# One activation and one multiply per tile in the middle of a gated-SiLU kernel, and its last tile stored in two pieces

## Chip, cores, metric

The kernel runs on one core of one Trainium2 chip. The metric is the device time of one execution in microseconds (us). An execution of this kernel repeats within about 0.3%. Tiles, loads and stores are numbered from 0.

## The reference

```python
def reference(x):                       # x: 32 x 512 x 2048, float32
    x1, x2 = x[..., :1024], x[..., 1024:]
    return (x1 * (1 / (1 + np.exp(-x1)))) * x2     # silu(x1) * x2
```

134.2 MB are read and 67.1 MB are written. There is one activation and one multiply for each output element, and nothing is used twice.

## The kernel before

The 16,384 rows are cut into 16 tiles of 1,024 rows: 128 partitions, 8 rows each. A tile of the input is 8.4 MB, a tile of the output 4.2 MB. Both pools have two buffers. Loads are issued from the scalar engine's (ACT's) queue, stores from the sync engine's (SP's) queue. Both kinds share the same 16 DMA engines.

```python
    K = 8
    KC = 2
    ...
    in_pool = ctx.enter_context(tc.tile_pool(name="in_pool", bufs=2))
    out_pool = ctx.enter_context(tc.tile_pool(name="out_pool", bufs=2))
    ...
    load(0)
    load(1)
    for i in range(n_tiles):
        ...
        last = i == n_tiles - 1
        ot = out_pool.tile([P, K, half], dt, name="ot")
        for c in range(0, k, KC):
            ce = min(c + KC, k)
            nc.scalar.activation(
                out=ot[:, c:ce, :],
                in_=xt[:, c:ce, :half],
                func=mybir.ActivationFunctionType.Silu,
            )
            nc.vector.tensor_mul(
                out=ot[:, c:ce, :],
                in0=ot[:, c:ce, :],
                in1=xt[:, c:ce, half:],
            )
            if last:
                nc.sync.dma_start(out=ov[:, c:ce, :], in_=ot[:, c:ce, :])
        if not last:
            nc.sync.dma_start(out=ov, in_=ot[:, :k, :])
        if i + 2 < n_tiles:
            load(i + 2)
```

So each tile is computed in four chunks of 2 rows: while the vector engine (DVE) multiplies one chunk, ACT computes the next. The store of a tile and the load of the tile after next are issued when the last multiply of the tile is done. The last tile is stored chunk by chunk.

Of the kernel before, what the change touches and what calls it, by code (L numbers as in the profile page):

```python
# [1 line left out]

# [4 lines left out]


def issue_ahead_of_the_first_barrier(nc):




    head, body = nc.main_func.blocks[:2]
    load = next(ins for ins in body.instructions if type(ins).__name__ == "InstDMACopy")
    at = next(
        j for j, ins in enumerate(head.instructions)
        if ins.engine == load.engine and type(ins).__name__ == "InstDrain"
    )
    body.instructions = [ins for ins in body.instructions if ins.name != load.name]  # L20
    head.instructions = head.instructions[:at] + [load] + head.instructions[at:]


@with_exitstack
def kernel(
    ctx: ExitStack,
    tc: tile.TileContext,
    x: bass.AP,
    out: bass.AP,
):  # L30






    nc = tc.nc
    P = nc.NUM_PARTITIONS

    x_flat = x.flatten_outer_dims()  # L40
    out_flat = out.flatten_outer_dims()
    num_rows, in_cols = x_flat.shape
    half = in_cols // 2
    dt = x_flat.dtype

    K = 8
    KC = 2
    PLAN = [K] * (num_rows // (P * K))

    in_pool = ctx.enter_context(tc.tile_pool(name="in_pool", bufs=2))  # L50
    out_pool = ctx.enter_context(tc.tile_pool(name="out_pool", bufs=2))

    plan = []
    row = 0
    for k in PLAN:
        plan.append((row, k))
        row += P * k
    assert row == num_rows
    n_tiles = len(plan)

    def view(flat, i):
        row0, k = plan[i]
        return flat[row0:row0 + P * k].rearrange("(p k) d -> p k d", k=k)

    nc.at_finalize(issue_ahead_of_the_first_barrier)


    ctx.enter_context(tc.manual_schedule())

    loaded = {}  # L70

    def load(i):
        xt = in_pool.tile([P, K, in_cols], dt, name="xt")
        nc.scalar.dma_start(out=xt[:, :plan[i][1], :], in_=view(x_flat, i))
        loaded[i] = xt
# [4 lines that stand above are left out]
        k = plan[i][1]  # L80
        xt = loaded.pop(i)
        last = i == n_tiles - 1
        ov = view(out_flat, i)
        ot = out_pool.tile([P, K, half], dt, name="ot")
        for c in range(0, k, KC):
            ce = min(c + KC, k)
            nc.scalar.activation(  # L87
                out=ot[:, c:ce, :],
                in_=xt[:, c:ce, :half],
# [4 lines that stand above are left out]
                in0=ot[:, c:ce, :],  # L94
                in1=xt[:, c:ce, half:],
            )
            if last:
                nc.sync.dma_start(out=ov[:, c:ce, :], in_=ot[:, c:ce, :])
        if not last:
            nc.sync.dma_start(out=ov, in_=ot[:, :k, :])  # L100
        if i + 2 < n_tiles:
            load(i + 2)


# [1 line left out]
_INS = ['x']  # L106
_OUTS = [((32, 512, 1024), 'float32')]


# [23 lines left out]
```

## Time and profile before

| | before |
|---|---|
| time, median of the first 3 runs | 470.82 us (470.62 to 471.04) |
| span of the profiled execution | 468.9 us |
| DVE busy, ACT busy | 142.3 us, 118.2 us |
| moved by DMA | 201.3 MB, 429 GB/s over the whole span |

First the windows view of the kernel before. A row gives a stretch of time from the start of the span, its length, each engine's busy us and instructions, the clock, the share of the time in which the 16 DMA engines were busy, and GB/s.

```profile
core 0: us, DVE busy (x) ACT busy (x) POOL busy (x), PEclk, DMA share, GB/s
50.00:79.00 29.00, 8.90 (x5) 7.32 (x6) 0.00 (x0) 1.00 1.00 434
400.00:429.00 29.00, 9.00 (x5) 7.41 (x5) 0.00 (x0) 1.00 1.00 434
454.00:460.00 6.00, 6.00 (x4) 4.34 (x3) 0.00 (x0) 1.00 0.91 389
```

Read the last two columns first. In the middle of the kernel the DMA engines are busy the whole time, at 434 GB/s, while DVE works 9 and ACT 7 of each 29 us. One tile's load and store are 12.6 MB, and 12.6 MB at 434 GB/s are these 29.0 us. The third row is the tail, after the last load has landed. A packet seems to be counted whole in the window in which it starts, since short windows can show a share above 1; so a window of a few us is only good to about a tenth.

The groups of instructions of the kernel before (line, engine, operation, output from input, shapes, count, busy us, mean ns, idle time before them and what ended it):

```profile
L92 DVE TENSOR_TENSOR ot<-ot,xt 128x2048 f32<-128x2048 f32 x64 | 142.3, 2286 | 319.5 <-ACT ot L87 319.5
L87 ACT ACTIVATE ot<-xt 128x2048 f32<-128x2048 f32 x64 | 116.9, 1897 | 338.8 <-DMA xt<-in_x_dram 338.8
```

The DMA issues of the kernel before (output from input, queue, count, size of one, median us from issue to landing):

```profile
out_dram<-ot SPq DMA_DIRECT2D x15, 4096.0 KB, 39.8
...
xt<-in_x_dram ACTq DMA_DIRECT2D x16, 47.1
```

A load needs 47.1 us from issue to landing although only 29.0 us of transfer lie behind it. The other 18.1 us it waits in the queue behind the load before it. This is the slack of the loads.

From the page of the kernel before, the chain that ended last, by line:

```profile
DMA xt<-in_x_dram 80%; DVE ot L92 15%; ACT ot L87 3%; DVEq L128 0%
```

And the timeline of the kernel before at the end (start, length, engine, line, instruction, count; in brackets the idle time before it and what ended it; four stores issued one after the other are one line):

```profile
451.03 7.31 ACT L87 ACTIVATE ot<-xt 128x2048 f32<-128x2048 f32 x4 [21.57 <-DMA xt<-in_x_dram]
452.97 8.90 DVE L92 TENSOR_TENSOR ot<-ot,xt 128x2048 f32<-128x2048 f32 x4 [19.98 <-ACT ot L87]
455.29 6.94 SPq L98 DMA_DIRECT2D out_dram<-ot  x4
```

The last load has landed at 451.0 us; the first chunk of the last tile is stored at 455.29 us, and all four are issued 6.94 us later.

The trace also records every DMA packet with its start and length. It does not say which of the 16 engines moved it, but packets of one engine follow each other without a pause, so the chains can be put together. Here is one such chain of the kernel before, by my own sorting (L a load packet of 64 KB, 2.42 us; s a store packet, 1.21 us for 32 KB and 0.31 us for 8 KB; the number is the start in us):

```
around store 0:  L33.26 L35.70 s38.88 L40.09 s42.50 s43.72 L44.93
in the tail:     s455.78 s457.00 s457.31 s457.61 s457.92 s458.22 ... s466.50   (from 457.00 on: the last tile)
```

Where both queues have work, load and store packets alternate. The two stores in a row at 42.50 are no exception: between them, at 43.71, the trace has a load packet of 4 bytes (9 ns). Every transfer ends with such an end packet on each engine (256 of them for 16 loads, 304 for 19 stores), and it takes a turn like any other. The Trainium skill, "DMA: Bandwidth & Descriptors", section "Queues, rings and completion order", says that each engine goes round the queues packet by packet; this trace agrees. From 1.1 us to 467.6 us no engine pauses.

### The profile page before, as it was taken

The numbers are of one execution on the slowest core, as the hardware profiler recorded it, in microseconds if no ns is written. First come the engines' busy times: TensorE is split into PE (matmuls) and PEld (weight loads), VectorE is DVE, ScalarE is ACT, GpSimd is POOL, SyncE is SP. The second block draws the span as 40 slices with busy tenths as digits, with TensorE's granted clock in tenths as the row PEclk, the third lists the DMA queues.
The fourth block names the chain that finished last, engine by engine and source line by source line (L and its number), as shares of the span: only waits on it lengthen the run. The fifth ranks groups of instructions, "written<-read, shape, count | busy, mean of one in ns | idle before, by whom it ended". The sixth has DMA issues, their size and how long they took to land.

```text
span 468.9 us, 269 instructions
## 1 busy us (share of the span) xinstructions
DVE 142.3 (30%) x64; ACT 118.2 (25%) x65; POOL 0.2 (0%) x4
## 2 busy tenths in 40 slices
DVE  0070705106061160601507025070250702407034
ACT  1142406023060330603206032060420604106051
POOL 0000000000000000000000000000000000000000
DMA  9899999999999998999999999999999989999998
GB/s 431 375 447 403 447 447 447 403 419 431 447 447 403 447 492 363 442 492 391 458 403 439 456 447 403 409 442 447 447 403 444 467 386 447 442 419 481 400 409 354
DMA packets 5042, 201.35 MB, mean 429 GB/s; under 512 B 560, under 2 KB 560, under 8 KB 560
## 3 DMA queue, kind: packets, MB, share of 16 engines
q10 hardware_dynamic: 2304, 134.22, 66.4%
q1 hardware_dynamic: 2736, 67.11, 33.2%
q14 instruction: 2, 0.02, 0.0%
HBM read 134.22 MB, written 67.11 MB: 429 GB/s over the span
## 4 chain that ended last, share of the span: by engine, by line
DMA 80%; DVE 15%; ACT 3%; DVEq 0%; issue 0%
DMA xt<-in_x_dram 80%; DVE ot L92 15%; ACT ot L87 3%; DVEq L128 0%
## 5 line engine op out<-in xcount | busy, mean ns | idle before, releaser
L92 DVE TENSOR_TENSOR ot<-ot,xt 128x2048 f32<-128x2048 f32 x64 | 142.3, 2286 | 319.5 <-ACT ot L87 319.5
L87 ACT ACTIVATE ot<-xt 128x2048 f32<-128x2048 f32 x64 | 116.9, 1897 | 338.8 <-DMA xt<-in_x_dram 338.8
L87 ACT ACT_TABLE_LOAD x1 | 1.3, 1283 | 1.3 <-PEq L117 1.3
L117 POOL MEMSET const-uint8-127<- 128x1 uint8 x1 | 0.1, 102 | 0.0
L117 POOL MEMSET const-bfloat16-1.0<- 128x1 bf16 x1 | 0.1, 101 | 0.0
L117 POOL MEMSET const-float32-0.0<- 128x1 f32 x1 | 0.1, 98 | 0.2 <-issue 0.2
L117 POOL MEMSET const-float32-1.0<- 128x1 f32 x1 | 0.1, 98 | 0.0
## 6 DMA issues: line engine op xcount, KB each, us to landing
out_dram<-ot SPq DMA_DIRECT2D x15, 4096.0 KB, 39.8
out_dram<-ot SPq DMA_DIRECT2D x4, 1024.0 KB, 5.7
xt<-in_x_dram ACTq DMA_DIRECT2D x16, 47.1
```

Source lines behind the costliest of these rows:

```text
L87: nc.scalar.activation(out=ot[:, c:ce, :], in_=xt[:, c:ce, :half], func=mybir.ActivationFunctionType.Silu,)
L92: nc.vector.tensor_mul(out=ot[:, c:ce, :], in0=ot[:, c:ce, :], in1=xt[:, c:ce, half:],)
L117: nc = _bacc.Bacc("TRN2", target_bir_lowering=False, num_devices=1)
```

## The change

The intent is fewer instructions: one activation and one multiply over all 8 rows in tiles 1 to 14, and fewer, larger stores at the end. The first tile keeps its four chunks; the last keeps its chunks too, but is stored in two pieces.

```diff
     K = 8
-    KC = 2
+    KC_EDGE = 2
+    KS = 4
...
-        for c in range(0, k, KC):
-            ce = min(c + KC, k)
+        kc = KC_EDGE if i in (0, n_tiles - 1) else k
+        for c in range(0, k, kc):
+            ce = c + kc
...
-            if last:
-                nc.sync.dma_start(out=ov[:, c:ce, :], in_=ot[:, c:ce, :])
+            if last and ce % KS == 0:
+                nc.sync.dma_start(out=ov[:, ce - KS:ce, :], in_=ot[:, ce - KS:ce, :])
```

## The prediction

> **What bounds it now.** The DMA engines, from end to end. The windows view gives 434 GB/s and a DMA share of 1.00 in every 29 us window that I asked for between 50 and 429 us, while DVE is busy 8.9 us and ACT 7.3 us of each. The Trainium skill, "DMA: Bandwidth & Descriptors", section "Where 436 GB/s comes from", puts the ceiling at 435.2 GB/s; the trace agrees. 201.3 MB at 434 GB/s is 464 us of the 468.9 us span. In the trace's DMA packets the 16 engines start at 1.1 us, never pause, and stop at 467.6 us. The chain of waits shows "DMA xt 80%, DVE 15%, ACT 3%", but the 18% are no cost: another load and a store are always queued.
>
> **Tiles 1 to 14.** Before, four activations (1.893 us each, 7.31 together) overlap four multiplies (2.284 each, 8.90 together): 10.85 us from a landed load to the issue of the store and of the load after next. After, they are in series. The Trainium skill, "ScalarE: Activation LUTs", section "What ACT_TABLE_LOAD costs", gives an activation 186 ns + 0.833 ns per element; for 2048 elements 1.892 (trace: 1.893), so 8192 take 7.0 us (estimate). The multiply: 8.90 less about three start-up costs, 8.5 to 8.8 us (estimate). Sum 15.7 us: busy time falls some 0.3 us on ACT and 0.2 us on DVE per tile, and each store and load is issued about 4.9 us later.
>
> **Critical path?** No, if the slack holds. Load i+1 starts moving when load i has landed and takes 29 us beside a store; so load i+2, issued 15.7 instead of 10.85 us after that landing, still has 13 us to spare. Stores: store 0 ends at 65.5 us in the packets, and store 1 is issued at 60.2 instead of 55.4 us, so the store queue keeps a backlog of 5.3 us, the same each tile. A transfer needs about 1.0 us from issue to first packet on free engines (first load), but store 0, issued into a busy queue, took 6.1 us. So the backlog may be just too short on some engines. Then a load packet (2.42 us) goes ahead of a store packet: no engine idles, loads land about 1.2 us earlier.
>
> **The tail.** The last load lands at 451.0; store 14 then occupies the engines until 457.0 to 457.8. Before, the first piece of tile 15 was issued at 455.3, in time. After, it needs two multiplies and is issued at 457.5; plus 1.0 us, it moves at about 458.5. So the engines idle about 1 us, once. Then 4.2 MB need 9.7 us; the second piece, issued at 461.9, comes before the first is through. End 468.4 instead of 467.6: about +0.8 us. If loads land 1.2 us early by the reordering above, the gap nearly vanishes: +0.1. I weigh the first more.
>
> **Prediction:** 471.5 us, range 470.7 to 472.4; faster by over 2%: 1%, within 2%: 97%, slower: 2%.
>
> **Right if:** middle windows still show 434 GB/s and loads land 29 us apart; ACT's mean in the middle tiles is near 7.0 us and DVE's near 8.7, with DVE's wait for ACT growing about 5 us a tile; the store's median issue-to-landing falls from 39.8 to about 35 us; the DMA share dips at 457 to 459 us.
>
> **Wrong if:** 128x8192 instructions cost more than linear; the later store lets engines run dry (DMA share under 1.00 in the middle); or one queue's packets run slower than two alternating ones.

## The result

| | before | after |
|---|---|---|
| time, median of 6 runs of the same rounds | 470.94 us (470.62 to 471.61) | 471.41 us (471.07 to 471.75) |
| ratio, 95% interval | | 1.0008 (0.9995 to 1.0021) |
| span of the profiled execution | 468.9 us | 469.4 us |
| DVE busy, ACT busy | 142.3, 118.2 us | 139.5, 114.3 us |
| instructions | 269 | 181 |

A ratio is the mean time of one kernel's runs over that of the other's of the same rounds, so not quite the ratio of the medians quoted. Here the interval contains 1; five more rounds in a later session (below) gave 1.0020 (1.0006 to 1.0033). So the changed kernel is slower, by 0.5 to 1.1 us in the medians.

The windows of the changed kernel, same columns and same stretches:

```profile
50.00:79.00 29.00, 8.69 (x1) 7.12 (x2) 0.00 (x0) 1.00 1.00 434
400.00:429.00 29.00, 8.69 (x1) 7.13 (x2) 0.00 (x0) 1.00 1.00 434
454.00:460.00 6.00, 6.00 (x4) 4.27 (x3) 0.00 (x0) 1.00 0.74 317
```

The middle is as it was: 434 GB/s, share 1.00. The tail is not: 0.74 instead of 0.91 between 454 and 460 us. The difference of 0.17 of 6 us is 1.0 us, good to a few tenths. The packets give the size more finely: the 16 engines stand idle for 0.85 us on the mean between 457 and 459 us, against none before. In the windows of just these 2 us, before and after:

```profile
457.00:459.00 2.00, 2.00 (x2) 1.34 (x1) 0.00 (x0) 1.00 0.95 401
457.00:459.00 2.00, 2.00 (x2) 1.27 (x1) 0.00 (x0) 1.00 0.60 254
```

The groups of the changed kernel, each shape by itself:

```profile
L94 DVE TENSOR_TENSOR ot<-ot,xt 128x8192 f32<-128x8192 f32 x14 | 121.7, 8692 | 283.1 <-ACT ot L89 283.1
L89 ACT ACTIVATE ot<-xt 128x8192 f32<-128x8192 f32 x14 | 98.4, 7029 | 301.2 <-DMA xt<-in_x_dram 301.2
L94 DVE TENSOR_TENSOR ot<-ot,xt 128x2048 f32<-128x2048 f32 x8 | 17.8, 2286 | 39.2 <-ACT ot L89 39.2
L89 ACT ACTIVATE ot<-xt 128x2048 f32<-128x2048 f32 x8 | 14.6, 1897 | 41.5 <-DMA xt<-in_x_dram 41.5
```

Four times the elements take 7.029 us on ACT and 8.692 us on DVE. In series that is 15.8 us with the hand-over, where the overlapped chunks had taken 10.9 us.

The DMA issues of the changed kernel:

```profile
out_dram<-ot SPq DMA_DIRECT2D x15, 4096.0 KB, 34.7
...
xt<-in_x_dram ACTq DMA_DIRECT2D x16, 42.2
```

Loads now land 42.2 us after their issue instead of 47.1. They were issued about 5 us later and landed within 0.6 us of the same times (the last at 450.94 instead of 451.00): of the 18.1 us of slack, 4.9 are used.

The chain that ended last, by line, from the page of the changed kernel:

```profile
DMA xt<-in_x_dram 72%; DVE ot L94 14%; ACT ot L89 11%; DVEq L130 0%
```

ACT's share went from 3% to 11% of the span. Whoever reads the chain as a list of costs would say that ACT became 36 us more costly (3.3% to 10.9% of 469 us before rounding). The time says half a microsecond. The chain follows one load, its tile's compute, the next load of the same buffer, and so on; it does not see that another load and a store kept the engines busy meanwhile.

The timeline of the changed kernel at the end:

```profile
450.96 7.31 ACT L89 ACTIVATE ot<-xt 128x2048 f32<-128x2048 f32 x4 [21.92 <-DMA xt<-in_x_dram]
452.90 8.90 DVE L94 TENSOR_TENSOR ot<-ot,xt 128x2048 f32<-128x2048 f32 x4 [15.14 <-ACT ot L89]
457.43 4.74 SPq L100 DMA_DIRECT2D out_dram<-ot  x2
```

The last load lands at the same time (450.96), but the first store of the last tile is issued at 457.43 us, after two multiplies, instead of at 455.29. One engine's packets (my sorting again, the same engine number as before has no meaning):

```
around store 0:  L33.51 L35.92 s39.20 L40.41 s42.83 s44.04 L45.25
in the tail:     s456.13 (ends 457.34)   s458.33 s458.95 s459.56 ...           (from 458.33 on: the last tile)
```

The engines run dry between 457.3 and 457.8 us, and each starts again at about 458.3 us, 0.83 us after the issue. The last packet ends at 468.25 us against 467.63 us before, 0.62 us later; the span is 0.52 us longer. The end moves by less than the 0.85 us of the gap mainly because the engines now finish together: they stand idle for 0.09 us on the mean before the last one ends, against 0.53 us before.

### The profile page after: what moved, and what is told of

It reads as the page before. It is cut to its first block, busy times and chain, and to the rows that moved or that the text cites. A ratio compares the mean times of both kernels' runs of the same rounds, so it can differ in the third digit from the quotient of the medians.

```text
span 469.4 us, 181 instructions
## 1 busy us (share of the span) xinstructions
DVE 139.5 (30%) x22; ACT 114.3 (24%) x23; POOL 0.2 (0%) x4
## 4 chain that ended last, share of the span: by engine, by line
DMA 72%; DVE 14%; ACT 11%; DVEq 0%; issue 0%
DMA xt<-in_x_dram 72%; DVE ot L94 14%; ACT ot L89 11%; DVEq L130 0%
## 5 line engine op out<-in xcount | busy, mean ns | idle before, releaser
L94 DVE TENSOR_TENSOR ot<-ot,xt 128x8192 f32<-128x8192 f32 (+1 forms) x22 | 139.5, 6363 | 322.3 <-ACT ot L89 322.3
L89 ACT ACTIVATE ot<-xt 128x8192 f32<-128x8192 f32 (+1 forms) x22 | 113.0, 5163 | 342.7 <-DMA xt<-in_x_dram 342.7
## 6 DMA issues: line engine op xcount, KB each, us to landing
out_dram<-ot SPq DMA_DIRECT2D x15, 4096.0 KB, 34.7
xt<-in_x_dram ACTq DMA_DIRECT2D x16, 42.2
```

The costliest lines, as they stand in the source:

```text
L89: nc.scalar.activation(out=ot[:, c:ce, :], in_=xt[:, c:ce, :half], func=mybir.ActivationFunctionType.Silu,)
L94: nc.vector.tensor_mul(out=ot[:, c:ce, :], in0=ot[:, c:ce, :], in1=xt[:, c:ce, half:],)
```

## The experiments

Two parts were changed at once, so there are two suspects. My theory is that the middle is free, because its later issues only use slack, and that the whole cost is the gap in the tail, made by the later first piece. The rival is that the later issues of the middle cost the half microsecond, and the two pieces nothing. All edits below are against the changed kernel.

### The middle merge alone

```diff
-    KS = 4
+    KS = 2
```

> The middle merge alone: tiles 1 to 14 with one activation and one multiply, the last tile stored in four pieces of 2 rows as before. Theory (the whole cost is a gap of about 0.8 us on the DMA engines at 457 to 459 us, made by the later first piece of the last tile): the first piece is issued at about 455.2 us, before store 14 has left the engines (about 457.5), so no gap; the time equals the kernel before, ratio 0.9995 to 1.0005, profiled span about 468.9 us. Rival (the 4.9 us later stores and loads of the middle cost the half microsecond, and the pieces are harmless): ratio about 1.001, span about 469.4 us.

Measured: 470.65 us against 470.80 us for the kernel before, ratio 0.9999 (0.9987 to 1.0012); profiled span 468.6 us. In the tail of this run, by its windows view and its timeline:

```profile
454.00:460.00 6.00, 6.00 (x4) 3.99 (x3) 0.00 (x0) 1.00 0.88 377
```

```profile
454.95 6.94 SPq L100 DMA_DIRECT2D out_dram<-ot  x4
```

The share is 0.88, near the 0.91 of before. The first piece is issued at 454.95 us, before store 14 has left the engines, and the packets show no pause. The interval alone would still allow half a microsecond either way; with the trace, and with the repeat on another chip, the middle merge is free as far as can be measured.

> The middle merge alone, repeated as the partner of the run before: equals the kernel before within 0.2 us, as it did.

Measured: 470.80 us against 470.71 us, ratio 0.9999 (0.9987 to 1.0012).

### The two pieces alone

```diff
-        kc = KC_EDGE if i in (0, n_tiles - 1) else k
+        kc = KC_EDGE
```

> The tail alone: every tile computed in four chunks of 2 rows as before, the last tile stored in two pieces of 4 rows. Theory: same gap as in the changed kernel, engines idle for 0.7 to 1.0 us on the mean between 457 and 459 us, span about 469.4 us, ratio about 1.001. Rival (the middle costs): ratio 1.000, span 468.9 us, no gap.

Measured: 471.64 us against 470.80 us, ratio 1.0019 (1.0006 to 1.0031); profiled span 469.6 us. Windows and timeline of its tail:

```profile
454.00:460.00 6.00, 6.00 (x4) 4.43 (x3) 0.00 (x0) 1.00 0.74 317
```

```profile
457.59 4.73 SPq L100 DMA_DIRECT2D out_dram<-ot  x2
```

The same 0.74 as in the changed kernel, with a middle that was not touched. The rival falls: the pieces make the loss. The changed kernel itself was run once more beside the middle merge alone.

> The changed kernel, repeated on the same chip as the middle merge alone: about 0.6 us above it (the gap in the tail) if the theory holds, no difference if the pieces are harmless.

Measured: 471.81 us, against 470.80 us for the middle merge alone and 470.71 us for the kernel before; ratio to the latter 1.0020 (1.0006 to 1.0033). The difference of 1.0 us is somewhat larger than the 0.6 us expected; the profiled execution of this run (span 469.3 us) was again 0.5 us over the partner's 468.8 us. What makes the other executions of this kernel, and those of the two pieces alone (spans of 469.8 to 470.2 us), some tenths longer than the profiled ones is not shown.

### Is it the gap, and does its size fit? The last tile in one piece

```diff
-    KS = 4
+    KS = 8
```

> The changed kernel with the last tile stored in one piece of 8 rows, issued at about 461.9 us after the fourth multiply. Theory, in size: the engines are empty from 457.5 on and start again 0.9 us after the issue, at about 462.7 us, so idle about 5.2 us; then 9.7 us for 4.2 MB; the end is about 472.4 instead of 467.6 us, span about 473.7 us, that is 4.8 us over the kernel before, ratio about 1.010. Rival (a fixed cost of larger pieces or packets, not the gap): at most another half microsecond, ratio about 1.002.

Measured: 475.83 us against 470.80 us, ratio 1.0113 (1.0098 to 1.0129); profiled span 473.4 us. Its tail by windows:

```profile
458.00:462.00 4.00, 3.49 (x2) 0.00 (x0) 0.00 (x0) 1.00 0.00 0
462.00:472.00 10.00, 0.00 (x0) 0.00 (x0) 0.00 (x0) 1.00 0.98 419
```

```profile
461.52 0.33 SPq L100 DMA_DIRECT2D out_dram<-ot  x1
```

Between 458 and 462 us nothing moves. The store is issued at 461.52 us and its first packets start at about 462.4 us; the last packet ends at 472.26 us, 4.6 us after that of before (4.8 were expected). So the loss follows from when the first piece is issued, and not from a fixed cost of larger pieces. Their packets are not dearer either: by packet lengths the last tile is 9.9 us of one engine's time in four pieces (packets of 8 KB) and in two (16 KB), and 9.8 us in one (32 KB).

### A slower kernel without the gap: 7 us more work in tile 1

If the gap is the cause, it must vanish when store 14 lasts longer or the last load lands sooner. That can be had by a delay. In this kernel tile 1 runs its activation twice (the values are the same).

```diff
-            nc.scalar.activation(
-                ...
+            for _ in range(2 if i == 1 else 1):
+                nc.scalar.activation(
+                    ...
```

> The changed kernel (two pieces) with one extra 7.0 us of work: tile 1 runs its activation twice, same values. Store 1 is then issued at about 67.7 us, after store 0 has left the engines (65.7 to 66.3 us). Theory (order on the queues, and the gap at the tail): the store queue is empty for a moment, load packets go ahead, no engine idles, the loads land at least one store packet per engine (1.2 us) earlier from then on, so the first piece is issued at 456.3 us or sooner, the gap at 457 to 459 us vanishes, and the slower kernel is the faster one: span about 468.8 us, ratio about 1.000 against 1.001 for the changed kernel. Rival (later stores cost time): ratio 1.001 or more, up to 1.016 if all 7 us count.

Measured: 470.64 us against 470.89 us for the kernel before, ratio 0.9993 (0.9981 to 1.0006). The changed kernel, with 7 us less work and the same two pieces, had 471.41 and 471.81 us (in other sessions, beside 470.94 and 470.71 us for the kernel before). By the timeline, load 3, which is issued together with store 1, and tile 2; then the tail by timeline and by windows:

```profile
68.26 0.37 ACTq L75 DMA_DIRECT2D xt<-in_x_dram  x1
71.79 7.03 ACT L90 ACTIVATE ot<-xt 128x8192 f32<-128x8192 f32 x1 [12.28 <-DMA xt<-in_x_dram]
```

```profile
448.95 7.31 ACT L90 ACTIVATE ot<-xt 128x2048 f32<-128x2048 f32 x4 [22.00 <-DMA xt<-in_x_dram]
...
455.41 4.74 SPq L101 DMA_DIRECT2D out_dram<-ot  x2
```

```profile
454.00:460.00 6.00, 5.79 (x3) 2.26 (x2) 0.00 (x0) 1.00 0.98 423
```

Tile 1 was done at 68.26 us, when store 0 had already left the engines (66.6 us at the latest). One engine's packets there read "L63.65 L66.07 L68.49 s70.91": three load packets in a row, no pause. In the changed kernel there are only two at this place ("L63.38 L65.80 s68.21"), with the end packet of store 0 between them; the third is the one that went ahead. From then on all loads land about 2 us sooner, the last at 448.95 instead of 450.96 us. About 1 us of this is the data (on one engine the last load's data end at 447.92 instead of 448.86 us). The rest is the load's end packet, which now follows its data at once, while in the changed kernel it waits 1.21 us for a store packet to pass. The stores have the same bytes left to move, so at that moment more of store 14 is still to be done, and it covers the wait for the first piece, issued at 455.41 us. The share in the tail is 0.98. The delay cost nothing, and the order that it caused removed the gap.

### How much slack is there? Two and three activations in each middle tile

Both kernels have four pieces in the tail (`KS = 2`), and repeat the activation in tiles 1 to 14.

```diff
+            for _ in range(2 if 0 < i < n_tiles - 1 else 1):     # or 3
```

> Tiles 1 to 14 merged with the activation run twice (compute of 22.8 us a tile in series instead of 15.8 or 10.85), last tile in four pieces. 98 us of extra ACT work. Theory (loads have about 29 us less one start-up of slack): DMA share stays 1.00 in the middle, loads run ahead once and then land 29 us apart, ratio 0.999 to 1.001. Rival (each us of later issue costs something): if the 4.9 us cost 0.5 us, 12 us cost about 1.2 us, ratio 1.0025; if the slack is shorter than I think, several us a tile.

Measured with two: 470.78 us against 470.89 us, ratio 0.9995 (0.9981 to 1.0008). 98 us more of ACT work are free.

```profile
50.00:79.00 29.00, 8.69 (x1) 16.87 (x4) 0.00 (x0) 1.00 1.01 436
400.00:429.00 29.00, 8.69 (x1) 14.03 (x3) 0.00 (x0) 1.00 1.00 434
```

ACT's busy time doubled, the DMA columns did not move. Its loads land 35.1 us after the issue: 6.1 us of slack are left.

> The same with three activations: 29.8 us of compute in series, just over the 29.0 us that a load and a store take together. Theory: now the next load and the store are issued together, after the engines have run out of both; each pair of tiles takes 29.8 us plus about 1.0 us of start plus 29 us, so about 30.2 us a tile instead of 29.0, in sum 10 to 20 us longer: 480 to 491 us, DMA share about 0.96 in the middle. If the time stays at 471, the slack is larger than the theory says; if it is above 500, something other than the slack costs.

Measured with three: 502.14 us, ratio 1.0662 (1.0642 to 1.0681). This is 31 us more, where I had expected 10 to 20; the slack does end where the theory says, but the price beyond it is higher. Only two executions were timed, 501.75 and 502.54 us, which is ample for a difference of this size. A part of the chain that ended last in this run, then two lines of its timeline, then two windows:

```profile
137.03 0.02 issue
137.05 32.09 DMA xt<-in_x_dram
169.13 0.02 issue
169.16 7.04 ACT ot L90
```

```profile
74.96 0.37 ACTq L75 DMA_DIRECT2D xt<-in_x_dram  x1
75.44 21.15 ACT L90 ACTIVATE ot<-xt 128x8192 f32<-128x8192 f32 x3 [9.23 <-DVE ot L95]
```

```profile
199.00:228.00 29.00, 7.27 (x2) 21.09 (x3) 0.00 (x0) 1.00 1.00 411
261.00:290.00 29.00, 7.32 (x2) 21.09 (x3) 0.00 (x0) 1.00 0.99 405
```

A load now takes 32.1 us from its issue, and compute plus load of one buffer take 62.1 us for two tiles, so 31.0 us a tile; 14 times 2.0 us are 28 of the 31 us. What I had missed are two things. The smaller: the load's issue stands in ACT's own queue and waits there for the multiply. After the issue at 74.96 us, the activation of tile 2 starts at 75.44 us, though its data had been there since 71.4 us, so activation and multiply of neighbouring tiles do not overlap. In the later pairs this costs little, since the load itself lands only about when the multiply ends (137.50 and 137.03 us). The larger: when new transfers start after the queues have run empty, with or without a pause of the engines between, the first packets are long: a store packet 1.5 to 2.0 us instead of 1.21, the load packet after it 3.0 to 3.6 us instead of 2.42, about 1.4 us for each tile. Summed over the trace, the packets of one engine take 486.0 us instead of 466.8, and the pauses are 13.3 us instead of 0.8. So of the 31.7 us by which the span is longer, about 19 are longer packets, and 12.5 are pauses. The pauses alone would have been within the 10 to 20 us that I expected; why the first packets are long is not shown. The share of busy DMA time stays at about 1.00 in these windows, since such a packet counts as busy; only the GB/s column (411 and 405) shows the loss. My expectation of a share of 0.96 was wrong for that reason.

### The other end: tile 0

In tile 0 there is no store yet, and only load 1 is on the engines. Merging tile 0 too delays load 2 and store 0.

```diff
-        kc = KC_EDGE if i in (0, n_tiles - 1) else k
+        kc = KC_EDGE if last else k
```

> The changed kernel with tile 0 merged too (only the last tile keeps four chunks), two pieces of 4 rows. Tile 0 is then through at about 37.7 instead of 33.0 us, so store 0 and load 2 are issued about 4.8 us later. Theory: no engine idles for that, because load 1 runs until 40 us and load 2 is queued by then; the loads run ahead of the stores and land about 1.5 us earlier for the rest of the kernel, last load about 449.4 us; so the first piece is issued at about 455.9 us, in time, the gap vanishes, and the span is 468.9 us, ratio 1.000, although more compute is in series. Rival (later stores and loads cost time): tile 0 adds its own delay, ratio 1.001 or above, up to 1.01 if the start is on the critical path.

Measured: 471.21 us (470.63 to 471.68) against 470.80 us, ratio 1.0009 (0.9996 to 1.0021). The profiled execution did as the theory says: the last load landed at 448.4 us, 2.6 us sooner (I had expected 1.5; by the packets it is two store packets per engine instead of one), there was no gap, and its span, 468.4 us, is the shortest of all profiled ones. But the other four executions have spans of 469.0 to 469.5 us. With four pieces in the tail, this was tried twice more.

> Tile 0 merged as well as tiles 1 to 14, and the last tile in four pieces of 2 rows. Only the timed median of the run with tile 0 merged and two pieces (1.0009, while its profiled execution was the fastest of its five) is unexplained: either tile 0's later store costs up to 0.4 us in most executions, or that was the scatter. Theory (free): ratio 0.9995 to 1.0005, span about 468.6 us, last load landing near 447.9 us. Rival (tile 0 costs): ratio about 1.001.

Measured: 471.29 us against 470.89 us, ratio 1.0007 (0.9994 to 1.0019).

> A repeat beside the middle merge alone on the same chip, to see whether merging tile 0 costs the 0.4 us that two runs showed in most executions but not in the profiled one. If it costs: 0.3 to 0.6 us over the middle merge alone in the medians. If it was scatter of the chip: within 0.15 us of it.

Measured: 471.59 us, beside 470.80 us for the middle merge alone on the same chip; executions of 470.84 to 471.71 us. Three runs of the same sign on three chips: merging tile 0 seems to cost some 0.5 us in most executions. Each of the three intervals contains 1 by itself, but together 11 of 15 executions took more than 471.1 us, against 3 of 27 of the kernel before in the same sessions. The profiled executions show no pause of the engines and have no such loss (span 468.7 us in both), so where it lies is not shown. The theory's "free" did not hold for tile 0, by this half microsecond.

The last run puts the 7 us of extra work into the merged tile 0 instead of tile 1. Beside the line shown, its edit has `KS = 2` and `kc = KC_EDGE if last else k`.

```diff
+            for _ in range(2 if i == 0 else 1):
```

> Tile 0 merged and its activation run twice (7.0 us more, once, in tile 0 instead of tile 1), last tile in four pieces. Load 2 and store 0 are then issued at about 44.8 us, when load 1 has already left the engines at about 41 us. Theory (a delay is free only while another transfer is queued): here nothing is queued, the engines idle from about 41 to 45.8 us, and the end is 4 to 5 us later: ratio 1.008 to 1.011. The same 7 us in tile 1 were free. Rival (one tile's delay of 7 us is free wherever it stands, since the loads catch up): ratio 1.000 to 1.002.

Measured: 478.16 us (476.74 to 479.96), ratio 1.0158 (1.0130 to 1.0186). The profile of this run:

```profile
45.05 0.37 SPq L103 DMA_DIRECT2D out_dram<-ot  x1
45.06 0.36 ACTq L75 DMA_DIRECT2D xt<-in_x_dram  x1
```

```profile
40.00:50.00 10.00, 5.03 (x1) 4.54 (x1) 0.00 (x0) 1.00 0.52 157
50.00:79.00 29.00, 8.69 (x1) 4.25 (x2) 0.00 (x0) 1.00 1.00 434
```

Load 2 and store 0 are issued at 45.05 us, the engines had been empty since about 40.6 us and start again at 46.0 us. Of the 5.7 us that this execution's span is longer than that of before (474.5 against 468.9 us), most is this pause. The same 7 us that were free in tile 1 cost here, because nothing else was queued. The loss is above the 4 to 5 us that I expected: the pause is 5.3 us on the mean of the engines, and the packets after it are long, as in the run before with three activations (0.7 us in all for one engine). Two of the four executions were another 2.6 to 3.2 us longer, which lifts the mean ratio to 1.0158 where at most 1.011 was expected; no profile shows why, and this stays open.

### Is there a better version?

No run beats the kernel before outside the noise. The packets say why: one engine's own packets, 128 load packets of 2.418 us, 120 store packets of 1.213 us and 32 of 0.309 us, are 465.0 us. The span of before is 468.9 us. Everything that this schedule could still save is under 4 us, and of that 1.1 us are the start of the first load and 1.3 us the end after the last packet. The middle merge with four pieces has the fewer instructions at the same time.

## Why the prediction was right

- **The bound.** Right: 434 GB/s in the middle windows of both kernels, share 1.00. The Trainium skill, "DMA: Bandwidth & Descriptors", section "Where 436 GB/s comes from", names 435.2 GB/s as the ceiling of the 16 ports; both traces agree with it. The same section also says that between HBM and the core's SBUF the HBM side binds at about 358 GB/s; in these traces of a single core it does not: loads and stores together run at 434 GB/s.
- **The merged instructions.** Right: predicted 7.0 and 8.5 to 8.8 us, measured 7.029 and 8.692 us. The formula of "ScalarE: Activation LUTs", section "What ACT_TABLE_LOAD costs", gives 7.010 us for 8192 elements; the trace is within 0.3% of it.
- **The middle is off the critical path.** Right, and shown by the middle merge alone (0.9999, twice) and by the doubled activation (0.9995). Loads landed 29.0 us apart in both profiles; the store's issue-to-landing fell to 34.7 us (predicted about 35).
- **The reordering.** It was named as possible and weighed less. It did not happen in the changed kernel: a backlog of about 5 us in the store queue was enough. It did happen with 7 us more.
- **The tail.** Right: first packets of the last tile predicted at 458.5 us, measured at 458.3; end at 468.4, measured 468.25. The term that was a little off is the start of a transfer on free engines: 1.0 us was used, from the first load, and 0.83 us was measured. So +0.8 us became +0.62 us in the packets and +0.52 us in the span.
- **One item of "Right if" failed.** I wrote that DVE's wait for ACT would grow by about 5 us a tile. It went from 319.5 us in all to 322.3 us (283.1 + 39.2). That column counts all idle time before a multiply, and puts it down to what ended it; DVE is idle for the rest of each 29 us whatever ACT does.

The time, 471.41 us, lay 0.1 us from the predicted 471.5 us. Part of that is luck: five later executions had a median of 471.81 us.

## What to carry to other kernels

When the DMA engines are busy from end to end, ask of each change first: does it ever leave the engines without a queued transfer? Read the slack from the median time from issue to landing less the time of the transfer itself (here 47.1 less 29.0), spend it in the middle but not to its end (7 us more in each tile where 6.1 us were left cost 31 us), and keep the fine chunks at the two ends, where nothing else is queued. A chain of waits that moves from 3% to 11% for an engine is no cost as long as the GB/s of the same stretch stay at the ceiling.

## What the Trainium skill lacked or had wrong

- "DMA: Bandwidth & Descriptors", section "Latency and other measured facts", gives about 600 ns to the first byte for transfers issued from the sync or scalar engine. Here it was 0.83 us from the issue to the first packet on idle engines in the tail, and 1.0 us for the first load of the kernel. The page has nothing on an issue into busy engines: store 0, issued beside a running load queue, saw its first packet 6.1 us later (32.74 to 38.88 us).
- No page tells what it costs when an empty queue starts. In the traces, the load packet just before store 0 took 3.2 to 3.6 us instead of 2.42, about 0.9 us on each engine; where both queues had run empty, a store packet took up to 2.0 us instead of 1.21 and the next load packet up to 3.6 us, which came to 19 us in the kernel with three activations. It happened in some restarts and not in others (none in tile 1 of the kernel with its activation doubled there, where only the store queue was empty).
- "DMA: Bandwidth & Descriptors", section "Measured (HBM→SBUF, 128 partitions, SWDGE, issued from GpSimd)", gives 6.15 us and 78% of the peak for a transfer of 1 MB, and advises batches of 1 MiB and more. Both sizes of piece here meet that, and it does not tell them apart. Here stores of 1 MiB that were queued behind each other ended 2.45 us apart, 428 GB/s, and the larger pieces were the slower choice.
- "DMA: Bandwidth & Descriptors", section "SWDGE vs HWDGE vs iDMA", calls packets of at most 4096 bytes preferable, in a table on transfers issued from GpSimd, and gives no size in bytes for those issued from SP and ACT as here. What the records here count as one packet is 65,536 bytes for loads and 32,768 for most stores, at the full 434 GB/s.
